# A one-core decoder layer: activation blocks stored 288 columns apart instead of 264, in 21 shared buffers instead of 23

## The chip, the cores and the metric

The kernel runs on one core of a Trainium2 chip. The metric is the device time of one execution in microseconds (us). Three runs of the kernel before took 2701.3, 2703.62 and 2700.91 us, so the median is 2701.3 us.

## What is computed

One layer of a hybrid decoder on 264 tokens: 256 of a prompt and 8 single tokens of running requests, all with 2,048 features and in float32. The reference, cut to what matters:

```python
def layer_forward(x, pos, ret_state0, ret_chunk, sparse_attn, p):
    x = x + 0.5 * swiglu(rms_norm(x, ffn1_norm), ffn1_w1, ffn1_w2)
    h = rms_norm(x, mix_norm)
    rq, rk, rv, rg, aq, ak, av, iq, ik, iw, g_ret, g_att = split_cols(h @ w_in)
    ret_out, ret_state = retention(rq, rk, rv, rg, ret_state0, ...)
    att = sparse_attn(rms_norm(aq), rms_norm(ak), av, iq, iw, ik)
    merged = sigmoid(g_ret) * ret_out + sigmoid(g_att) * (att @ w_att_out)
    x = x + merged @ w_o
    x = x + 0.5 * swiglu(rms_norm(x, ffn2_norm), ffn2_w1, ffn2_w2)
    return x, ret_state, ak, av, ik
```

Every weight is read once from DRAM, and nearly all the arithmetic is the products of weights with the activations of the 264 tokens.

## The kernel before, in words

Features lie on the 128 partitions and tokens along the row, so an activation block is [128 features, 264 tokens], 1,056 bytes in each partition. Four such blocks make one **quad**, a tile [128, 4, 264] from `qpool`, a pool of `NQ` = 23 buffers that nearly every larger tile shares (`quad`, L146; `Blocks`, L166, hands out block `i` as `[:, i % 4, :]` of quad `i // 4`). The residual X (4 quads), the two halves of the normalized input of a stage (`hi` and `lo`, 4 quads each), the two halves of the hidden features of an FFN chunk (`hh`, `hl`), the quads of retention and attention (`rk`, `rq`, `vr`, `ro`, `kn`, `qn`) and, with other shapes of at most 4,100 bytes, the tiles of the decode tokens' side work (`sb`, `kq`, `kv`, `kb`, `qb`, `pr`) all come from it. A tile that wants a buffer waits until the last reader of the buffer's previous tile is done.

`mblock` (L236) multiplies 128 columns of a weight matrix with up to 16 activation blocks. For each 8 rows of blocks it loads 512 KB of weights (`wr`, SyncE's queue), rounds them on ScalarE to float32r (`wh`, L247), takes the rest on VectorE, or in some stages on GpSimd (`wl`, L248), and then issues per block k three TensorE matmuls of 264 columns: L251 with moving block `hi[k]` and weights `wh`, L252 with `lo[k]` and `wh`, L253 with `hi[k]` and `wl`. `wr`, `wh` and `wl` have four buffers each. There are 20,400 such matmuls in the program.

The stages in order: FFN 1 (`ffn`, L305: three chunks of hidden features, each all of its `w1` blocks, then all of its `w2` blocks), the combined projection (`mixblock`, in the order iq, rk, rq, rv, ak, av, aq, gr, ga, rg), the three products with `wro`, `wao` and `wo`, and FFN 2. Between the blocks of the combined projection Python generators are stepped (`step`, L411) that hold the side work: the index search, prompt attention, retention, and for the 8 decode tokens `retention_decode` (L889) and `decode_attention` (L788). `retention_decode` has 16 steps: load a state `sb` and two broadcasts `kq` on ScalarE's queue, `kv` and the update of `sb` on VectorE, a product on GpSimd (L905), a sum on VectorE (L906), and the store of `sb`. `decode_attention` has 16 half steps: a broadcast `qb` on ScalarE's queue, two products `pr` on GpSimd (L802) and their sums on VectorE (L804), with `kb` gathered once per two.

The framework's scheduler orders each engine's instructions by priority and its own estimate of time, and it decides which of the free buffers a tile gets.

In each partition's memory the pools lie one behind the other in the order in which they are made, and tiles are rounded up to 32 bytes. In the built program of before the first quad lies at byte 26,688, which is 64 past a multiple of 128. A quad takes 4,224 bytes, 33 times 128, so every quad begins 64 past a multiple of 128, and the four blocks of a quad begin 64, 96, 0 and 32 bytes past one. All `wh` and `wl` blocks (512 bytes each) begin 64 past one.

Of the kernel before, what the change touches and what calls it, by code (L numbers as in the profile page):

```python
# [9 lines left out]
F32 = mybir.dt.float32  # L10
# [6 lines left out]
PSUM = bass.MemoryType.PSUM  # L17
DRAM = bass.MemoryType.DRAM

P = 128  # L20
# [2 lines left out]
TP = 256  # L23
NB = 8
T = TP + NB
FF = 5632
FB = FF // P
CHUNKS = ((0, 16), (16, 32), (32, 44))
EPS = 1e-6
# [13 lines left out]
SW = 136  # L43
# [5 lines left out]
ORDER = (("iq", 8), ("rk", 8), ("rq", 8), ("rv", 16), ("ak", 4), ("av", 4), ("aq", 16), ("gr", 16), ("ga", 16),  # L49
         ("rg", 16))  # L50

NQ = 23
AHEAD = 1500

CC = {}
_c = 0
for _n, _w in (("ident", 128), ("cos", T), ("sin", T), ("causal", 384), ("kdec", 16), ("bm8", 8), ("rep", 128),
               ("pages", 16), ("same", 128), ("before", 128), ("eighths", 7), ("slot", 2), ("segkey", 1),
# [63 lines left out]
def layer(ctx: ExitStack, tc: tile.TileContext, xT, gains, consts, dmat, didx, pt, state, cidx, ck, cv,  # L122
# [6 lines left out]
    cpool = ctx.enter_context(tc.tile_pool(name="cpool", bufs=1))  # L129
    qpool = ctx.enter_context(tc.tile_pool(name="qpool", bufs=NQ))  # L130
    rawp = ctx.enter_context(tc.tile_pool(name="rawp", bufs=4))
    hip = ctx.enter_context(tc.tile_pool(name="hip", bufs=4))
    lop = ctx.enter_context(tc.tile_pool(name="lop", bufs=4))
    work = ctx.enter_context(tc.tile_pool(name="work", bufs=2))
# [7 lines left out]
    def nm(s):  # L142
        cnt[0] += 1
        return f"{s}_{cnt[0]}"

    def quad(dt=F32, shape=(P, 4, T), s="q"):  # L146
        return qpool.tile(list(shape), dt, tag="q", name=nm(s))

    def quads(n, dt=F32, s="q"):
        return [quad(dt, s=s) for _ in range(n)]  # L150

    def wt(s="w", shape=(P, T), dt=F32, tag="w", bufs=8):
        return work.tile(list(shape), dt, tag=tag, name=nm(s), bufs=bufs)

    def mt(s, shape=(P, 384), dt=F32):
        return work.tile(list(shape), dt, tag="m", name=nm(s), bufs=8)
# [4 lines left out]
    def aux():  # L161
        return psa.tile([P, 512], F32, tag="aux", name=nm("aux"))

    def auxm():
        return psa.tile([P, 512], F32, tag="auxm", name=nm("auxm"), bufs=1)

    class Blocks:
# [3 lines left out]
        def __getitem__(self, i):  # L171
            q = i // 4
            if q not in self.t:
                self.t[q] = quad(self.dt, s=self.s)
            return self.t[q][:, i % 4, :]
# [27 lines left out]
    nc.vector.memset(ones256, 1.0 / 256)  # L203
    ones1 = cpool.tile([P, P], F32, name="ones1")
    nc.vector.memset(ones1, 1.0)
    onesw = cpool.tile([P, SW], F32, name="onesw")
    nc.vector.memset(onesw, 1.0)
    epst = cpool.tile([P, 1], F32, name="epst")
    nc.vector.memset(epst, EPS)

    ptb = cpool.tile([P, NB, NPG], I32, name="ptb")
# [9 lines left out]

    xs = dpool.tile([P, KB, T], F32, name="xs")
    gs = dpool.tile([2, KB, P, T], F32, name="gs")
    ats = dpool.tile([P, AH, TP], F32, name="atsd")
# [3 lines left out]
    rows = dpool.tile([3, P, P], F32, name="rows")  # L228
# [7 lines left out]
    def mblock(src, nk, hi, lo, m=P):  # L236
        ps = psm.tile([P, 512], F32, tag="ps", name=nm("ps"))
        for c0 in range(0, nk, 8):
# [10 lines left out]
            for k in range(n):  # L249
                g = c0 + k  # L250
                nc.tensor.matmul(ps[:m, :T], wh[:, k, :m], hi[g], start=g == 0, stop=False)  # L251
                nc.tensor.matmul(ps[:m, :T], wh[:, k, :m], lo[g], start=False, stop=False)  # L252
# [3 lines left out]
    def root(ms, y, t):  # L256
        nc.scalar.activation(t, ms, AF.Ln)
        nc.scalar.activation(y, t, AF.Exp, scale=-0.5)

    def newton(y, ms, t):  # L260
        nc.vector.tensor_tensor(t, y, y, op=ALU.mult)
        nc.vector.scalar_tensor_tensor(t, t, -0.5, ms, op0=ALU.mult, op1=ALU.mult)
        nc.vector.scalar_tensor_tensor(y, t, 1.5, y, op0=ALU.add, op1=ALU.mult)

    def rsqrt(src, y, ms, t):
        """y = (src + EPS) ** -0.5"""
        nc.vector.tensor_scalar(ms, src, EPS, None, op0=ALU.add)
        root(ms, y, t)
        newton(y, ms, t)

    class Norm:
        """Gains and sums of squares of the blocks of x as they come; the mean's root follows at the evacuations."""

        def __init__(self, gain):
            self.gain = cc(gain)
# [17 lines left out]
        def done(self):  # L293
            ps = auxm()
            nc.tensor.matmul(ps[:, :T], onesD, self.acc, start=True, stop=True)
            ms, t = wt("ms"), wt("t")
            self.rstd = wt("rstd", tag="rstd", bufs=2)
            rsqrt(ps[:, :T], self.rstd, ms, t)
            return self.rstd
# [53 lines left out]
    ffn(norm, w1a, w2a, out1, early=1)  # L353

    KT = [[quad(shape=(P, 1024 + h), s="kt") for h in range(2)] for _ in range(4)]
    kt_order = [(p, 8 * h + i) for h in range(2) for p in range(4) for i in range(8)]

# [11 lines left out]
    blocks = {}  # L369
# [281 lines left out]
    VSELF = st([P, KVH, NB], tag="vself", bufs=1)  # L651

    def rms_roots(sums):
        """Steps from functions that give PSUM sums to the tiles of two roots each."""
        ss, y, t = (mt(n, (P, 2, T)) for n in ("ss", "y", "t"))
        for j, f in enumerate(sums):
            pq = aux()
            f(pq[:, :T])
            nc.scalar.activation(ss[:, j, :], pq[:, :T], AF.Identity, bias=epst)
        yield  # L660
        root(ss, y, t)
        yield
        newton(y, ss, t)
        yield y

    def norm_heads(raw, gain, i):
        """Normalizes two of the four heads of a quad in place."""
        sq = []
        for j in range(2):
            q = wt("sq")  # L670
            nc.scalar.activation(q, raw[:, i + j, :], AF.Square)
            sq.append(q)
        yield

        def total(j):
            return lambda pq: nc.tensor.matmul(pq, ones128, sq[j], start=True, stop=True)

        for y in rms_roots([total(0), total(1)]):
            yield
        r = raw[:, i:i + 2, :]  # L680
        nc.vector.scalar_tensor_tensor(r, r, gain, y, op0=ALU.mult, op1=ALU.mult)
        yield

    def k_task():
        for i in (0, 2):
            yield from norm_heads(KN.t[0], cc("gk"), i)
        nc.scalar.dma_start(o_k, KN.t[0])
        nc.vector.tensor_copy(KS, KN.t[0][:, :, TP:])
        yield
        KG = quad(s="kg")  # L690
        nc.scalar.activation(KG, KN.t[0], AF.Copy, scale=gqs)
        KN.t[0] = KG
        yield
# [12 lines left out]
    QR = st([P, AH, 2], tag="qr", bufs=1)  # L706

    def q_task(g):
        """Means of squares of four heads, with the tokens on the partitions."""
        pq = aux()  # L710
        for i in range(4):
            q = wt("sq")
            nc.scalar.activation(q[:, :TP], QN[4 * g + i][:, :TP], AF.Square)
            for tt in range(2):
                c = 2 * i + tt
                nc.tensor.matmul(pq[:, c:c + 1], q[:, P * tt:P * tt + P], ones128[:, :1], start=True, stop=True)
            if i % 2:
                yield
        nc.vector.tensor_copy(QSS[:, 4 * g:4 * g + 4, :].rearrange("p h t -> p (h t)"), pq[:, :8])
        nc.vector.tensor_copy(QS[:, 4 * g:4 * g + 4, :], QN.t[g][:, :, TP:])  # L720
        yield
# [151 lines left out]
        nc.gpsimd.tensor_add(out, a, b)  # L873

    def bcast_rows(src, which, scale=1.0):
        """src [128 d, (b, h)] as rows of d in DRAM, to be read onto all partitions."""
        n = src.shape[1]
        pr = auxm()
        nc.tensor.transpose(pr[:n, :P], src, ident)
        rt = mt("rt", (P, P))  # L880
        nc.scalar.activation(rt[:n], pr[:n, :P], AF.Copy, scale=scale)
        nc.scalar.dma_start(rows[which, :n], rt[:n])
# [73 lines left out]
    def group_norm():  # L956
        for hq in range(4):
            sq = {}
            for i in range(2):
                for e in range(2):  # L960
                    q = wt("sq")
                    nc.scalar.activation(q, RO[2 * (2 * hq + i) + e], AF.Square)
                    sq[i, e] = q
            yield

            def total(i):
                def f(pq):
                    for e in range(2):
                        nc.tensor.matmul(pq, ones256, sq[i, e], start=e == 0, stop=e == 1)
                return f  # L970

            for y in rms_roots([total(0), total(1)]):
                yield
            for i in range(2):
                h = 2 * hq + i
                for e in range(2):
                    nc.vector.scalar_tensor_tensor(RO[2 * h + e], RO[2 * h + e], cc("grn")[:, e:e + 1], y[:, i, :],
                                                   op0=ALU.mult, op1=ALU.mult)
            yield
# [98 lines left out]
    for i in range(16):  # L1078
# [3 lines left out]
        s = wt("s")  # L1082
# [56 lines left out]


def _blocks(w):
    """[K, M] as [M / 128, 128, K / 128, 128]: the columns' blocks, each with its rows on the partitions."""
    k, m = w.shape
    return np.ascontiguousarray(w.reshape(k // P, P, m // P, P).transpose(2, 1, 0, 3))

# [58 lines left out]
```

## Time and profile before, and how to read it

| what | value |
|---|---|
| median of three runs | 2701.3 us |
| profiled execution, its span | 2703.1 us |
| TensorE matmul busy | 2621.5 us, 97% of the span, 21,205 instructions |
| VectorE busy | 1596.6 us, 59% |
| ScalarE busy | 1163.4 us, 43% |
| GpSimd busy | 647.2 us, 24% |
| mean granted TensorE clock | 0.987 |

For the profiled execution no time of its own is given beside its span of 2703.1 us; the three runs lie within 2.8 us of one another, and the span lies 1.8 us above their median. Engines in the rows: PE is TensorE's matmuls, PEld its weight loads, DVE is VectorE, ACT ScalarE, POOL GpSimd, SP SyncE; a letter q behind a name is that engine's queue of transfers. L251 is line 251 of the kernel. The records of one matmul overlap the next ones, because matmuls are pipelined: the time that a matmul takes from the engine is read from one start to the next and not from its own duration. [...]

### The profile page before, as it was taken

How to read it: one execution, taken by the hardware profiler on the slowest of the kernel's cores; microseconds unless marked ns; L12 is line 12 of the kernel's file. 1: busy time of each engine (PE TensorE's matmuls, PEld its weight loads, DVE VectorE, ACT ScalarE, POOL GpSimd, SP SyncE). 2: the span in 40 equal slices, each digit the busy share in tenths (PEclk: the TensorE clock that was granted, in tenths of full speed). 3: DMA queues.
4: the chain of work that ended last, by engine and by line, in shares of the span. 5: the costliest groups of instructions: out<-in, count | busy, mean ns of one | idle time of the engine just before them, and what ended most of it. 6: DMA issues, size and time to landing. Idle time of an engine off the chain costs nothing.

```text
span 2703.1 us, 51188 instructions
## 1 busy us (share of the span) xinstructions
PE 2621.5 (97%) x21205; PEld 2588.8 (96%) x21205; DVE 1596.6 (59%) x2301; ACT 1163.4 (43%) x1551; POOL 647.2 (24%) x427
## 2 busy tenths in 40 slices
PE   7999999999999899999988899999999999999999
PEld 7999999999999699899988899999999999999999
DVE  6555555555566578568798845566655555554554
ACT  5443344334453333443545654444544334433443
POOL 3110011001127443445455543231111001100110
PEclk9999999999999899998998999999999999999999
DMA  6556555655566354468886666666555655566555
GB/s 216 180 181 184 181 180 181 184 182 180 173 218 214 108 170 157 141 213 282 266 291 228 203 195 223 206 208 210 180 181 182 181 183 180 180 181 183 181 166 173
DMA packets 164745, 520.67 MB, mean 193 GB/s; under 512 B 21680, under 2 KB 38640, under 8 KB 164512
## 3 DMA queue, kind: packets, MB, share of 16 engines
q1 hardware_dynamic: 126496, 445.31, 52.4%
q10 hardware_dynamic: 32112, 56.51, 6.4%
q0 software_dynamic: 5904, 15.59, 1.8%
q8 instruction: 166, 2.72, 0.4%
q14 instruction: 67, 0.55, 0.1%
HBM read 495.73 MB, written 21.60 MB: 191 GB/s over the span
## 4 chain that ended last, share of the span: by engine, by line
PE 82%; DVE 7%; issue 3%; DMA 3%; POOL 2%; ACT 2%; ACTq 0%; DVEq 0%; POOLq 0%
PE ps L252 27%; PE ps L251 26%; PE ps L253 26%; DVE wl L248 2%; DMA wr<-win 1%; POOL wl L248 1%; POOL pr L802 1%; DVE junk L534 1%; ACT wh L247 1%; DMA qb<-rows 0%; DMA kq<-rows 0%; DMA vb<-cv,rowi 0%; DVE sTs L804 0%; PE aux L443 0%; DVE sb L903 0%
## 5 line engine op out<-in xcount | busy, mean ns | idle before, releaser
L247 ACT ACTIVATE wh<-wr 128x1024 fp32r<-128x1024 f32 x866 | 902.0, 1043 | 1294.1 <-PE ps L252 838.5
L248 DVE TENSOR_TENSOR wl<-wr,wh 128x1024 fp32r<-128x1024 f32 (+2 forms) x798 | 990.3, 1241 | 740.2 <-ACT wh L247 739.1
L251 PE MATMUL ps<-hi,wh 128*128 128x264 f32 x4624 | 1326.4, 287 | 19.3 <-ACT hi L282 10.1
L253 PE MATMUL ps<-hi,wl 128*128 128x264 f32 x4624 | 1326.7, 287 | 16.2 <-DVE wl L248 13.3
L252 PE MATMUL ps<-lo,wh 128*128 128x264 f32 x4624 | 1329.2, 287 | 1.6 <-DVE lo L283 1.5
L251 PEld LDWEIGHTS ps<-hi,wh 128*128 128x128 f32 x4624 | 878.0, 190 | 23.0 <-ACT hi L282 10.1
L253 PEld LDWEIGHTS ps<-hi,wl 128*128 128x128 f32 x4624 | 876.1, 189 | 24.6 <-DVE wl L248 16.1
L252 PEld LDWEIGHTS ps<-lo,wh 128*128 128x128 f32 x4624 | 877.0, 190 | 8.7 <-issue 5.3
L322 POOL TENSOR_TENSOR s<-s,rstd 128x264 f32<-128x264 f32 x88 | 127.5, 1449 | 1252.6 <-ACT s L320 1252.6
L253 PE MATMUL ps<-hh,wl 128*128 128x264 f32 x1408 | 399.0, 283 | 0.0
L252 PE MATMUL ps<-hl,wh 128*128 128x264 f32 x1408 | 398.7, 283 | 0.0
L251 PE MATMUL ps<-hh,wh 128*128 128x264 f32 x1408 | 398.5, 283 | 0.0
L252 PEld LDWEIGHTS ps<-hl,wh 128*128 128x128 f32 x1408 | 264.7, 188 | 0.0
L251 PEld LDWEIGHTS ps<-hh,wh 128*128 128x128 f32 x1408 | 264.6, 188 | 0.0
L253 PEld LDWEIGHTS ps<-hh,wl 128*128 128x128 f32 x1408 | 264.4, 188 | 0.0
L248 POOL TENSOR_TENSOR wl<-wr,wh 128x1024 fp32r<-128x1024 f32 x68 | 170.2, 2508 | 289.9 <-ACT wh L247 250.4
L802 POOL TENSOR_TENSOR pr<-qb,kb 128x1024 f32<-128x1024 f32 x32 | 93.4, 2937 | 57.9 <-DMA qb<-rows 23.5
L291 POOL TENSOR_TENSOR acc<-acc,sq 128x264 f32<-128x264 f32 x45 | 40.5, 900 | 153.7 <-ACT sq L290 152.7
L329 DVE TENSOR_TENSOR h<-ps,s 128x264 f32<-128x264 f32 x88 | 38.0, 432 | 66.0 <-PE ps L253 62.7
L362 POOL DMA_INDIRECT kt<-cidx,kix x64 | 71.9, 1123 | 19.1 <-issue 18.5
L252 PE MATMUL ps<-mlo,wh 128*128 128x264 f32 x256 | 72.9, 285 | 0.0
L252 PE MATMUL ps<-alo,wh 128*128 128x264 f32 x256 | 72.7, 284 | 0.0
(311 smaller groups left out, 2270.0 us busy)
## 6 DMA issues: line engine op xcount, KB each, us to landing
wr<-win SPq DMA_DIRECT2D x224, 512.0 KB, 4.4
wr<-w1a SPq DMA_DIRECT2D x176, 512.0 KB, 3.8
wr<-w1b SPq DMA_DIRECT2D x176, 512.0 KB, 3.7
wr<-w2a SPq DMA_DIRECT2D x80, 512.0 KB, 3.7
wr<-w2b SPq DMA_DIRECT2D x80, 512.0 KB, 3.6
wr<-wro SPq DMA_DIRECT2D x32, 512.0 KB, 4.8
wr<-wao SPq DMA_DIRECT2D x32, 512.0 KB, 4.9
wr<-wo SPq DMA_DIRECT2D x32, 512.0 KB, 3.9
```

Source lines behind the costliest of these rows:

```text
L247: nc.scalar.activation(wh[:, :n, :m], wr[:, :n, :m], AF.Copy)
L248: eng.tensor_sub(wl[:, :n, :m], wr[:, :n, :m], wh[:, :n, :m])
L251: nc.tensor.matmul(ps[:m, :T], wh[:, k, :m], hi[g], start=g == 0, stop=False)
L252: nc.tensor.matmul(ps[:m, :T], wh[:, k, :m], lo[g], start=False, stop=False)
L253: nc.tensor.matmul(ps[:m, :T], wl[:, k, :m], hi[g], start=False, stop=g == nk - 1)
L291: nc.gpsimd.tensor_add(self.acc, self.acc, sq)
L322: nc.gpsimd.tensor_mul(s2, s, rstd)
L329: nc.vector.tensor_mul(h, pu, s2)
L362: nc.gpsimd.indirect_dma_start(out=KT[p][pg // 8][:, o:o + PG], out_offset=None, in_=cidx, in_offset=bass.IndirectOffsetOnAxis(ap=kix[:, p ...
L534: nc.vector.scalar_tensor_tensor(junk, VS, thr, onesw, op0=ALU.is_ge, op1=ALU.mult, accum_out=out)
L802: nc.gpsimd.tensor_mul(pr, qb, k.to_broadcast([P, 2, 4, P]))
```

## The change

`quad` without a shape now takes a tile [128, 4, 288] and hands out its first 264 columns; the pool has 21 buffers. `onesw` takes 24 columns more, and `epst` goes from `cpool` into a new pool of 64 bytes between `wr` and `wh`, which shifts the addresses of what follows. Comments between triple quotes go, without effect.

```diff
 T = TP + NB
+TS = 288
...
-NQ = 23
+NQ = 21
...
     rawp = ctx.enter_context(tc.tile_pool(name="rawp", bufs=4))
+    offp = ctx.enter_context(tc.tile_pool(name="offp", bufs=1))
     hip = ctx.enter_context(tc.tile_pool(name="hip", bufs=4))
...
-    def quad(dt=F32, shape=(P, 4, T), s="q"):
+    def quad(dt=F32, shape=None, s="q"):
+
+        if shape is None:
+            return qpool.tile([P, 4, TS], dt, tag="q", name=nm(s))[:, :, :T]
         return qpool.tile(list(shape), dt, tag="q", name=nm(s))
...
-    onesw = cpool.tile([P, SW], F32, name="onesw")
+    onesw = cpool.tile([P, SW + 24], F32, name="onesw")[:, :SW]
     nc.vector.memset(onesw, 1.0)
-    epst = cpool.tile([P, 1], F32, name="epst")
+    epst = offp.tile([P, 16], F32, name="epst")[:, :1]
```

In the built program the first quad now lies at byte 26,752, a multiple of 128, a quad takes 4,608 bytes, 36 times 128, and a block 1,152, 9 times 128. So all 20,400 moving blocks begin on a multiple of 128. The `wh` and `wl` blocks begin 64 past one, as before. Matmuls still read 264 columns.

The scheduler's order moves where quads are scarce. First ScalarE's queue in the aq stage, at the seventh and eighth of the 16 steps of `retention_decode` (sb is the state's tile, o_sts the output that it is stored to, sq belongs to attention). Before:

```order
L894 DMA sb_14360<-state 128x1024
L898 DMA kq_14362<-rows 128x512 x2
L713 ACTIVATE sq_14513<-qn_14277 128x256
L247 ACTIVATE wh_14438<-wr_14437 128x1024
L247 ACTIVATE wh_14468<-wr_14467 128x1024
L713 ACTIVATE sq_14517<-qn_14277 128x256
L894 DMA sb_14498<-state 128x1024
L898 DMA kq_14500<-rows 128x512 x2
L908 DMA o_sts<-sb_14360 128x1024
```

The same place with the change (line numbers are 5 higher):

```order
L899 DMA sb_14363<-state 128x1024
L903 DMA kq_14365<-rows 128x512 x2
L718 ACTIVATE sq_14516<-qn_14280 128x256
L252 ACTIVATE wh_14441<-wr_14440 128x1024
L252 ACTIVATE wh_14471<-wr_14470 128x1024
L718 ACTIVATE sq_14520<-qn_14280 128x256
L913 DMA o_sts<-sb_14363 128x1024
L252 ACTIVATE wh_14561<-wr_14560 128x1024
L899 DMA sb_14501<-state 128x1024
L252 ACTIVATE wh_14591<-wr_14590 128x1024
L903 DMA kq_14503<-rows 128x512 x2
```

The load of the next state moved from ahead of the store of the last one to behind it, and `kq` with it. Second, GpSimd at the eighth to eleventh step and the first products of `decode_attention` (kv and pr are the products, kb a gathered page). Before:

```order
L905 TENSOR_TENSOR kv_14503<-sb_14498,kq_14500 128x1024
L782 DMA kb_14875<-ck,rowi_12896 128x512 x2
L905 TENSOR_TENSOR kv_14716<-sb_14711,kq_14713 128x1024
L802 TENSOR_TENSOR pr_14880<-qb_14878,kb_14875 128x1024
L802 TENSOR_TENSOR pr_14883<-qb_14878,kb_14875 128x1024
L802 TENSOR_TENSOR pr_15049<-qb_15047,kb_14875 128x1024
L905 TENSOR_TENSOR kv_14891<-sb_14886,kq_14888 128x1024
L802 TENSOR_TENSOR pr_15052<-qb_15047,kb_14875 128x1024
```

With the change:

```order
L910 TENSOR_TENSOR kv_14506<-sb_14501,kq_14503 128x1024
L910 TENSOR_TENSOR kv_14719<-sb_14714,kq_14716 128x1024
L787 DMA kb_14878<-ck,rowi_12899 128x512 x2
L807 TENSOR_TENSOR pr_14883<-qb_14881,kb_14878 128x1024
L807 TENSOR_TENSOR pr_14886<-qb_14881,kb_14878 128x1024
L910 TENSOR_TENSOR kv_14894<-sb_14889,kq_14891 128x1024
L807 TENSOR_TENSOR pr_15052<-qb_15050,kb_14878 128x1024
L807 TENSOR_TENSOR pr_15055<-qb_15050,kb_14878 128x1024
```

The two kinds of products, which were interleaved one by one, now follow each other in whole pairs. SyncE's order, the weight loads, is the same in both, and so is nearly all of TensorE's.

## Rows read from the trace of the kernel before

**Rows 1.** The page: the span, and each engine's busy time, share and instructions.

```profile
span 2703.1 us, 51188 instructions
PE 2621.5 (97%) x21205; PEld 2588.8 (96%) x21205; DVE 1596.6 (59%) x2301; ACT 1163.4 (43%) x1551; POOL 647.2 (24%) x427
```

**Rows 2.** Busy time by stretch: stretch, length, engines' busy us (instructions), clock, DMA share, GB/s.

```profile
60.00:790.00 730.00, 730.00 (x6031) 730.00 (x6030) 383.13 (x446) 305.82 (x373) 70.94 (x55) 1.00 0.60 183
790.00:1530.00 740.00, 679.54 (x5180) 653.03 (x5179) 553.59 (x1050) 317.45 (x484) 377.64 (x213) 0.95 0.64 208
1530.00:2690.00 1160.00, 1157.45 (x9599) 1153.04 (x9599) 617.18 (x745) 501.69 (x632) 176.99 (x129) 1.00 0.60 189
```

**Rows 3.** TensorE in order of time, FFN 1, from a quad's first block: start, duration, what.

```profile
300.20 0.28 PE L251 MATMUL ps<-hi,wh 128*128 128x264 f32 x1
...
300.56 0.29 PE L251 MATMUL ps<-hi,wh 128*128 128x264 f32 x1
...
300.93 0.28 PE L251 MATMUL ps<-hi,wh 128*128 128x264 f32 x1
301.05 0.28 PE L252 MATMUL ps<-lo,wh 128*128 128x264 f32 x1
301.16 0.28 PE L253 MATMUL ps<-hi,wl 128*128 128x264 f32 x1
301.28 0.28 PE L251 MATMUL ps<-hi,wh 128*128 128x264 f32 x1
...
301.65 0.28 PE L251 MATMUL ps<-hi,wh 128*128 128x264 f32 x1
```

**Rows 4.** The same view, the first quad of the product with wro.

```profile
1650.42 0.28 PE L251 MATMUL ps<-rhi,wh 128*128 128x264 f32 x1
...
1650.78 0.28 PE L251 MATMUL ps<-rhi,wh 128*128 128x264 f32 x1
...
1651.14 0.29 PE L251 MATMUL ps<-rhi,wh 128*128 128x264 f32 x1
...
1651.51 0.28 PE L251 MATMUL ps<-rhi,wh 128*128 128x264 f32 x1
...
1651.86 0.28 PE L251 MATMUL ps<-rhi,wh 128*128 128x264 f32 x1
```

**Rows 5.** The same view, the first quad of the product with wo.

```profile
1836.46 0.28 PE L251 MATMUL ps<-mhi,wh 128*128 128x264 f32 x1
...
1836.83 0.29 PE L251 MATMUL ps<-mhi,wh 128*128 128x264 f32 x1
...
1837.19 0.28 PE L251 MATMUL ps<-mhi,wh 128*128 128x264 f32 x1
...
1837.54 0.28 PE L251 MATMUL ps<-mhi,wh 128*128 128x264 f32 x1
...
1837.91 0.28 PE L251 MATMUL ps<-mhi,wh 128*128 128x264 f32 x1
```

**Rows 6.** Waits from 1180 to 1530 us: who for whom, us in total, times, longest.

```profile
ACT wh L247 <- DMA wr<-win: 32.1, 10, 6.9
...
POOL pr L802 <- DMA qb<-rows: 23.5, 6, 6.8
```

**Rows 7.** The chain that ended last: start, us, what; the first load, one of qb.

```profile
1.29 8.22 DMA x<-xT
...
1333.45 8.10 DMA qb<-rows
```

**Rows 8.** ScalarE's table loads by line: busy, mean ns.

```profile
L257 ACT ACT_TABLE_LOAD x10 | 12.8, 1283 | 2.6 <-DVE qm L1056 2.5
```

## The prediction

> **What bounds the kernel now.** I read the page first: TensorE's matmuls are busy for 97% of the span, no other engine for more than 59% [rows 1]. A busy TensorE can still be a slow one, so the second view is the busy time by stretch [rows 2]. From 60 to 790 us and from 1530 to 2690 us TensorE has next to no idle time, and the clock is granted in full: 6,031 matmuls in 730.00 us are 121.0 ns each, 9,599 in 1160.00 us are 120.8 ns. Almost all of them are the 264-column kind. [...] From 790 to 1530 us it is different: 5,180 matmuls take 740 us, and TensorE is idle for 60 us of them, while VectorE is at 75%. There the side work of the decode tokens sets the pace in places.
>
> [...] By the addresses given ahead, the four blocks of a quad begin 64, 96, 0 and 32 bytes past a multiple of 128, and each block is the moving operand of three matmuls in a row. From the first matmul of one block to that of the next, a quad in FFN 1 takes 0.36, 0.37, 0.35 and 0.37 us [rows 3]: the third block, the only one on a multiple of 128, is the quickest. In the product with wo it is 0.37, 0.36, 0.35, 0.37 [rows 5]. In the product with wro it is 0.36, 0.36, 0.37, 0.35 [rows 4]: there the aligned block is the slowest. Starts are given to 0.01 us, so the error of one such difference is as large as the differences; what speaks is that two of three places agree.
>
> **The change, part by part.** *All moving blocks on a multiple of 128.* The three aligned blocks took 0.35, 0.37 and 0.35 us, a mean of 0.357 us or 118.9 ns a matmul. Against the 121.0 ns of the stretches that is 2.1 ns. The bounds: if the FFN 1 block is what every block becomes, 0.35 / 3 = 116.7 ns, a gain of 4.3 ns; if the wro block is, 0.37 / 3 = 123.3 ns, a loss of 2.3 ns. I take the mean, since nothing in the rows says which of the three a program of aligned blocks alone is like. In the two stretches with a busy TensorE there are 15,630 matmuls: 15,630 x 2.1 ns = 32.8 us. Of the 5,180 between, I count half as on the path, since TensorE is near 92% busy there but waits for the side work at its ends: 2,590 x 2.1 = 5.4 us. Together 38 us less. Loading and splitting weights must keep up: VectorE is at 52% and 53%, ScalarE at 42% and 43%, DMA at 60% in those stretches [rows 2], so a TensorE that is 2% faster meets no other engine.
>
> *23 buffers become 21.* In an FFN the residual, the two halves of the input and the two halves of a chunk hold 4 + 8 + 8 = 20 quads. The first two quads of the next chunk then find one free buffer instead of three, but the last readers of the old ones are matmuls that stand ahead on TensorE anyway, so I cost this at nothing; what hides it is TensorE's own order. It differs around 1180 to 1530 us. With the normalized input (8), RO (4), QN (up to 4), the scaled keys and the values (2) held, 5 of 23 buffers are left for `sb`, `kq`, `kv`, `kb`, `qb`, `pr`; of 21 only 3. The order shows it: the load of a state moves behind the store of the last one, and GpSimd's products no longer alternate. What waits is ScalarE's queue, and behind the waiting transfer stand the roundings `wh`, and behind those `wl` and the matmuls. The price of one exposed load is that of qb, 8.1 us [rows 7]. Seven steps of `retention_decode` lie in the stretch where `decode_attention` wants buffers too, so the cost lies between nothing (the four `wh` buffers cover 11.6 us of TensorE, four times 24 matmuls of 121 ns) and 7 x 8.1 = 57 us. That side work already waits here for loads, 23.5 us at `pr` alone, and the roundings wait 32.1 us for weights [rows 6]. I take one exposed load, 8 us: nearer to nothing, because the order moves each load by a few roundings and not by a step.
>
> *The loads of x and the spills.* A quad's rows are no longer contiguous, so a transfer of 4,224 bytes in a partition becomes four of 1,056. The first load of x is on the path at the start with 8.22 us [rows 7]. Bounds: nothing, if the bytes set its time, and another 8.2 us if it doubles. I take 1 us, since the bytes are the same. The later spills and reloads run beside TensorE.
>
> *The rest.* ScalarE's order holds five more table loads, 1.28 us each [rows 8], 6.4 us on an engine that is idle for 422 of the 740 us in that stretch; nothing. The padding of `onesw` and the move of `epst` issue nothing. If that cover is gone, it is 6.4 us.
>
> **The sum.** 2703.1 - 38 + 8 + 1 = 2674 us for the profiled execution, which lies 1.8 us above the median of the runs: **2672 us**.
>
> **The rivals.** *R1, every block as quick as the aligned one in FFN 1.* For it: two of three places [rows 3, 5], and no block then follows a misaligned one. Against it: [rows 4]. 15,630 x 4.3 ns = 67 us and half of 5,180, 11 us: 2703.1 - 78 + 9 - 1.8 = 2632 us. Chance 0.22.
>
> *R2, the change of place does not change the rate.* Quads in the rows take 1.45 us however the four blocks share it: 1.45 in [rows 3], 1.44 in [rows 4], 1.45 in [rows 5], and the stretches agree to 0.2 ns a matmul. A quick block may only get back what its neighbours lost. The wro quad is also the one whose two halves lie a multiple of 256 bytes apart, as all do after the change (a quad is then 18 times 256). Then nothing is won, and the two costs remain, from 0 to 9 us and a little more: 2701 to 2712 us. [...] Chance 0.23.
>
> *R3, the buffers decide.* The mechanism is ScalarE's queue: a load of `sb` that waits for the store of the last state holds up `wh`, and with it TensorE. From more than about five exposed loads on (38 / 8.1 = 4.7) it eats the gain. With all seven: 2701.3 - 38 + 57 + 1 = 2721 us, slower. Chance 0.08.
>
> *R4, aligned blocks are slow when they are alone.* As in [rows 4] every block takes 0.37 us: 15,630 x 2.3 + 2,590 x 2.3 = 42 us more, and 9 us: 2752 us. Chance 0.07.
>
> [...]
>
> **How the numbers follow.** The forecast has 0.37, R1 0.22, R2 0.23, R3 0.08, R4 0.07, R5 0.03. The forecast's own range, with the buffers costing 0 to 25 us, is 2660 to 2690 us. The range that holds 8 in 10 takes in R1 with a little below and the lower part of R2's costs and above: 2620 to 2714 us; R5, R4 and most of R3 stay out. A measurement of this kernel tells about 0.2%, 5.4 us. Faster by more: the forecast, R1 and R5, and a little of R2: 0.64. Within: half of R2, 0.12. Slower: the rest of R2, R3 and R4, with a part of the forecast whose buffers cost more: 0.24.
>
> **What would show it.** In the stretches of FFN 1 and 2 the matmuls per us: 8.26 before, 8.41 in the forecast, 8.57 with R1, the same with R2, fewer with R4. TensorE in order of time: four equal blocks of a quad, 0.357 us each, and no block at 0.37. From 1180 to 1530 us: waits of ScalarE's `wh` for stores of `sb` (o_sts) in the forecast about 8 us, with R3 over 40. At the start, the load of x at 8 to 10 us. The forecast is wrong if the blocks of a quad still differ, if the matmuls per us do not move, or if the stretch from 790 to 1530 us gets longer by more than 15 us.

## The result, and the profile after

Four runs of the changed kernel took 2722.05 to 2728.57 us, median 2726.58 us; the kernel before took 2702.46 us (median of four) beside it. The ratio is 1.0081, its 95% interval 1.0067 to 1.0095: **24 us slower**, where 29 us faster was forecast (2672 us against 2701.3). That is above the range's upper end of 2714 us. The page of the changed kernel, to be held against [rows 1]:

```profile
span 2723.8 us, 51226 instructions
PE 2619.0 (96%) x21205; PEld 2585.5 (95%) x21205; DVE 1605.2 (59%) x2301; ACT 1169.0 (43%) x1556; POOL 640.9 (24%) x427
```

Engines are as busy as before, and the span is 20.7 us longer: the time went into waiting. Where it went is read from the matmuls that fit into the same stretches. Busy time by stretch, first of the changed kernel, then of the kernel before (stretch, length, TensorE's busy us and matmuls, weight loads, VectorE, ScalarE, GpSimd, granted TensorE clock with 1.00 for the full one, DMA share, GB/s):

```profile
60.00:790.00 730.00, 730.00 (x6030) 730.00 (x6029) 382.26 (x444) 305.62 (x372) 70.95 (x55) 1.00 0.61 183
790.00:1290.00 500.00, 465.37 (x3622) 445.34 (x3621) 339.68 (x776) 197.43 (x286) 236.59 (x151) 0.97 0.57 185
1290.00:1530.00 240.00, 197.89 (x1455) 191.62 (x1454) 204.24 (x251) 116.99 (x193) 118.68 (x54) 0.91 0.72 238
1530.00:1680.00 150.00, 140.68 (x1201) 135.09 (x1200) 82.20 (x149) 79.41 (x127) 65.93 (x47) 0.99 0.62 204
1700.00:2690.00 990.00, 990.00 (x8175) 989.93 (x8175) 533.24 (x596) 415.53 (x499) 122.20 (x88) 1.00 0.60 187
```

```profile
790.00:1290.00 500.00, 469.06 (x3612) 448.85 (x3611) 343.02 (x780) 197.75 (x285) 242.78 (x154) 0.97 0.58 186
1290.00:1530.00 240.00, 210.48 (x1571) 204.18 (x1570) 210.57 (x271) 119.70 (x200) 134.86 (x59) 0.93 0.77 254
1530.00:1680.00 150.00, 147.45 (x1282) 143.10 (x1282) 75.12 (x137) 79.60 (x126) 55.07 (x41) 1.00 0.63 203
1700.00:2690.00 990.00, 990.00 (x8154) 989.93 (x8153) 531.34 (x596) 413.69 (x496) 117.12 (x86) 1.00 0.60 187
```

In FFN 1 nothing moved: 6,030 matmuls against 6,031 in [rows 2], 121.1 ns each against 121.0. From 1290 to 1530 us there are 116 matmuls fewer, from 1530 to 1680 us 81 fewer; at 121 ns these are 14.0 and 9.8 us lost. From 790 to 1290 us ten more fit in, and in FFN 2 twenty-one more: 1.2 and 2.5 us won. The sum, 20.1 us, is the growth of the span to within 0.6 us. So the whole loss lies in the stretch where the decode tokens' side work runs, and where buffers are scarce.

The four blocks of a quad in FFN 1, TensorE in order of time, as in [rows 3]:

```profile
300.79 0.28 PE L256 MATMUL ps<-hi,wh 128*128 128x264 f32 x1
...
301.15 0.28 PE L256 MATMUL ps<-hi,wh 128*128 128x264 f32 x1
...
301.51 0.28 PE L256 MATMUL ps<-hi,wh 128*128 128x264 f32 x1
...
301.88 0.28 PE L256 MATMUL ps<-hi,wh 128*128 128x264 f32 x1
...
302.24 0.28 PE L256 MATMUL ps<-hi,wh 128*128 128x264 f32 x1
```

0.36, 0.36, 0.37 and 0.36 us: the blocks are equal now, to the 0.01 us of the starts, as the alignment lets one expect, but equal at the old mean. 1.45 us for the quad, as before. Over 82 quads in a row from there the four blocks take 120.6 to 121.7 ns a matmul in the changed kernel; over 82 quads from the first of [rows 3] they take 121.7, 121.7, 117.2 and 123.9 ns in the kernel before. The mean is 121.1 ns in both. (The rounding of the starts leaves an error of about 1 ns in such a mean by place.) So the third block of [rows 3] was quick indeed, and the others paid for it.

Waits from 1290 to 1530 us (who for whom: us in total, times, longest), changed kernel, then the kernel before:

```profile
POOL kv L910 <- DVE sb L908: 48.8, 7, 12.4
...
POOL pr L807 <- DMA qb<-rows: 41.3, 10, 9.9
...
PE ps L258 <- DVE wl L253: 16.7, 12, 4.1
...
DVE kv L906 <- DMA kq<-rows: 13.9, 7, 3.8
...
PE aux L974 <- ACT sq L967: 12.9, 1, 12.9
ACT sq L967 <- DVE ro L916: 10.3, 1, 10.3
...
PE ps L256 <- ACT wh L252: 8.6, 2, 6.2
```

```profile
POOL kv L905 <- DVE sb L903: 18.5, 3, 8.3
...
PE ps L253 <- DVE wl L248: 10.0, 7, 3.7
...
PE aux L969 <- ACT sq L962: 2.1, 1, 2.1
...
DVE kv L901 <- DMA kq<-rows: 0.8, 1, 0.8
```

GpSimd waits for the updated state (`sb`) 48.8 us instead of 18.5, for `qb` 41.3 instead of 23.5 [rows 6], VectorE for `kq` 13.9 instead of 0.8: the steps of the side work overlap less. (In all GpSimd is idle for 121 us of these 240 instead of 105; part of its longer waits were waits for something else before.) TensorE has no part in these steps until it needs a result. The largest single wait is there: the matmuls of the group norm (L974) need `ro`, which the fifteenth of the sixteen steps completes for half of the heads, and TensorE stands still for 12.9 us before them. The last sums of the two generators (`rd` of `retention_decode`, `sTs` of `decode_attention`; first and last start), before and after:

```profile
L906 DVE TENSOR_REDUCE rd<-kv x16: 1204/1207/1223, 1199.0 to 1449.1; 128x8 f32<-128x1024 f32 x16
...
L804 DVE TENSOR_REDUCE sTs<-pr x32: 1201/1206/1220, 1317.1 to 1523.5; 128x8 f32<-128x1024 f32 x32
```

```profile
L911 DVE TENSOR_REDUCE rd<-kv x16: 1204/1207/1223, 1200.3 to 1463.2; 128x8 f32<-128x1024 f32 x16
...
L809 DVE TENSOR_REDUCE sTs<-pr x32: 1197/1204/1221, 1317.7 to 1545.2; 128x8 f32<-128x1024 f32 x32
```

Both begin when they did and end 14 and 22 us later. The product with wro begins 23.0 us later (1673.4 us against 1650.4), and from there on nothing more is lost.

### The profile page after: what moved, and what is told of

Same layout as the page of the kernel before. It is cut to its first block, busy times and chain, and to the rows that moved or that the text cites. A ratio compares the mean times of both kernels' runs of the same rounds, so it can differ in the third digit from the quotient of the medians.

```text
span 2723.8 us, 51226 instructions
## 1 busy us (share of the span) xinstructions
PE 2619.0 (96%) x21205; PEld 2585.5 (95%) x21205; DVE 1605.2 (59%) x2301; ACT 1169.0 (43%) x1556; POOL 640.9 (24%) x427
## 3 DMA queue, kind: packets, MB, share of 16 engines
q10 hardware_dynamic: 35952, 56.51, 6.5%
q0 software_dynamic: 5904, 15.59, 1.7%
## 5 line engine op out<-in xcount | busy, mean ns | idle before, releaser
L807 POOL TENSOR_TENSOR pr<-qb,kb 128x1024 f32<-128x1024 f32 x32 | 86.9, 2734 | 56.0 <-DMA qb<-rows 48.4
```

Source lines behind the costliest of these rows:

```text
L807: nc.gpsimd.tensor_mul(pr, qb, k.to_broadcast([P, 2, 4, P]))
```

## The experiments

Times of the runs e1 to e11 stand beside 2703 to 2705 us of the kernel before on the same chip. From e12 on the chips were others, on which the kernel before itself took 2749 us (e12 to e15) and 2737 us (e16 to e18). In e13 much of the difference lies between 790 and 1280 us, where it does 3,244 matmuls at a mean granted clock of 0.93 and e1 does 3,557 at 0.97. There only ratios are read, and between runs on different chips of the others too.

### Buffers or layout: e1 to e4

e1, e2 and e3 change one number in the kernel before:

```diff
-NQ = 23
+NQ = 21      (e1; 22 in e2, 24 in e3)
```

e4 changes it in the changed kernel:

```diff
-NQ = 21
+NQ = 22
```

> The kernel before with 21 buffers of 4,224 bytes instead of 23, nothing else; blocks stay 264 columns apart. Theory A (the buffers cost the time, the layout changes nothing or wins a few us): the stretch from 1290 to 1510 us grows by about 22 us as in the changed kernel, 2722 to 2730 us in all, and GpSimd's waits at pr and kv double. Theory B (the padded layout itself costs the time, by its transfers or by the matmuls): near 2702 us.

> The kernel before with 22 buffers. Theory A with a cost by the buffer: half way, 2708 to 2718 us. Theory A with a threshold (the fourth free buffer is the one that is missed): 2701 to 2705 us, or as with 21. Theory C (not the number but the accident of the schedule's order decides): no order among 21, 22, 23 and 24 buffers.

> The kernel before with 24 buffers, one more than before; it fits in the 264-column layout. Theory A: faster than 2702 us by up to the step from 22 to 23, 2690 to 2700 us. Theory B: the same, 2702 us. Theory C: anything from 2690 to 2725 us.

> The changed kernel with 22 buffers of 4,608 bytes instead of 21; the order of instructions is all but the same as in the run with 22 buffers of 4,224 bytes, so the difference of those two is the layout alone. Theory A: within 6 us of that run, below it rather (the matmuls of FFN 2 ran at 120.8 ns before, and at about 0.2 ns less in the changed kernel, 2 to 4 us). Theory B: some 20 us above it. A gain as I forecast from alignment, 38 us, would be seen here without the cost of the buffers: it is not expected any more.

| kernel | us | ratio, 95% interval | last `sTs` | wro begins |
|---|---|---|---|---|
| 264 columns, 23 buffers (before) | 2703.8 | 1 | 1523.5 | 1650.4 |
| 288 columns, 21 (the change) | 2726.6 | 1.0081 [1.0067, 1.0095] | 1545.2 | 1673.4 |
| e1: 264 columns, 21 | 2726.7 | 1.0079 [1.0066, 1.0093] | 1543.4 | 1669.5 |
| e2: 264 columns, 22 | 2716.0 | 1.0037 [1.0024, 1.0051] | 1538.3 | 1670.6 |
| e4: 288 columns, 22 | 2721.6 | 1.0064 [1.0051, 1.0078] | 1529.1 | 1659.4 |
| e3: 264 columns, 24 | 2704.8 | 1.0007 [0.9998, 1.0016] | 1509.7 | 1649.0 |

(The change was measured beside 2702.5 us. The last two columns are us in the one profiled execution, which for e2 lies above and for e4 below the median of its runs.) e1 settles it: without padding or alignment, the two missing buffers alone give the changed kernel's time, 1.0079 against 1.0081. Theory B falls, and that the times follow the number of buffers speaks against the accident of theory C. One buffer fewer costs about half. A 24th wins nothing, where theory A had 2690 to 2700 us: the side work then ends 14 us sooner, and TensorE does not gain by it. What TensorE needed of the side work it has in time with 23. With 22 buffers the padded layout (e4) is 6 us slower than e2 by the medians, where theory A had it rather below; the two intervals just touch, and where the 6 us come from stays open.

### Does the place of a block matter at all: e8, e11, e12

e8 puts 32 bytes more in front of the quads of the changed kernel:

```diff
-    onesw = cpool.tile([P, SW + 24], F32, name="onesw")[:, :SW]
+    onesw = cpool.tile([P, SW + 32], F32, name="onesw")[:, :SW]
```

> The changed kernel (288 columns, 21 buffers) with 32 bytes more in front of the quads, so that all 20,400 moving blocks begin 32 bytes past a multiple of 128 and none on one. Theory neutral (the place of a block does not set the rate; quick blocks gave back what slow neighbours took): 6,030 matmuls in the stretch from 60 to 790 us again, 121.0 ns each, and 2722 to 2731 us in all. Theory place (a block on a multiple of 128 is quicker than one at 32, as 119.4 to 122.2 ns by place in the kernel before would have it): 5,975 matmuls or fewer, and 2740 us or more.

2728.1 us, ratio 1.0086 [1.0069, 1.0102]. (The blocks of `wh` and `wl` lie behind the quads and move by 32 bytes too, from 64 to 96 past a multiple of 128.) FFN 1 in e8 (all moving blocks at 32), and below it in e1 (264 columns, blocks at 0, 32, 64 and 96), the same view:

```profile
60.00:790.00 730.00, 730.00 (x6030) 730.00 (x6029) 382.31 (x444) 305.63 (x372) 70.98 (x55) 1.00 0.60 183
```

```profile
60.00:790.00 730.00, 730.00 (x6030) 730.00 (x6029) 382.99 (x446) 305.70 (x373) 70.92 (x55) 1.00 0.61 183
```

All at 0, all at 32, and mixed: 6,030, 6,030 and 6,030 matmuls. From 1700 to 2690 us the two equal layouts have 8,175 each and e1 has 8,167, but that is no effect of the layout: other kernels with mixed blocks have 8,154 (the one before) to 8,187 (e2). Nor does the rest of the program tell the layouts apart. From the first matmul of the product with wro to the end it takes 1048.9 to 1052.9 us in the nine kernels with 264 columns up to e10, and 1050.3 or 1050.4 us in the three with 288. The quick block of [rows 3] was quick at its neighbours' cost.

e11 and e12 shorten two of the three matmuls of each block in the changed kernel, and so leave the corrections out for a part of the tokens:

```diff
-                nc.tensor.matmul(ps[:m, :T], wh[:, k, :m], lo[g], start=False, stop=False)
-                nc.tensor.matmul(ps[:m, :T], wl[:, k, :m], hi[g], start=False, stop=g == nk - 1)
+                nc.tensor.matmul(ps[:m, :TP], wh[:, k, :m], lo[g][:, :TP], start=False, stop=False)
+                nc.tensor.matmul(ps[:m, :TP], wl[:, k, :m], hi[g][:, :TP], start=False, stop=g == nk - 1)
```

(TP is 256; e12 has P, 128, in its place.)

> The changed kernel with two of the three matmuls of each block (the corrections, lo with wh and hi with wl) reading 256 columns instead of 264: the corrections of the eight decode tokens are left out. [...] If the array takes a fixed time by the column (121.1 / 264): 118.65 ns, 6,152 matmuls. If whole lines of 128 bytes count (nine for 264 columns, eight for 256): (121.1 + 2 x 107.6) / 3 = 112.1 ns, 6,510 matmuls, and this would be the one way in which the place of a block could matter. If a matmul's issue sets the rate: 121.1 ns, 6,030 matmuls.

> As the run with 256 columns, but the two corrections read 128 columns: they are left out for the second half of the prompt and the decode tokens. [...] If a pair of weight load and matmul has a floor near 119 ns whatever its columns, 119 to 121 ns, and 6,030 to 6,130 matmuls from 60 to 790 us. If the second, narrower moving operand is read at a slower rate, 200 ns and more.

e11 took 2706.2 us. FFN 1 in e11, then in e12, busy time by stretch:

```profile
60.00:790.00 730.00, 730.00 (x6085) 729.93 (x6084) 387.20 (x450) 309.74 (x377) 71.64 (x56) 1.00 0.61 185
```

```profile
60.00:790.00 730.00, 721.99 (x6292) 721.05 (x6291) 400.28 (x467) 320.04 (x388) 92.55 (x77) 0.99 0.64 194
```

e11: 730.00 / 6,085 = 120.0 ns. If the long matmul still takes 121.1, the short ones take 119.4 ns: eight columns saved 1.6 ns, less than half of the 3.7 ns that are eight 264ths of 121.1. None of the three expectations holds. e12: 721.99 / 6,292 = 114.7 ns for a mean of 173 columns: a third of the columns gone, 5% of the time saved, at a mean granted clock of 0.99. Of its two expectations the floor near 119 ns comes nearer, and neither holds. (From 790 to 1530 us the mean granted clock in e12 is 0.63, against 0.95 in [rows 2], and its whole, 2852 us and more, tells nothing of a matmul.) But 115 ns is no floor under every pair of a weight load and its matmul. The 48 matmuls of the narrow product with `wik` have weights of 80 columns instead of 128. The first of them in e12, and the first of the sixteenth group of three, TensorE in order of time:

```profile
750.54 0.30 PE L256 MATMUL ps<-hi,wh 128*80 128x264 f32 x1
...
754.51 0.30 PE L256 MATMUL ps<-hi,wh 128*80 128x264 f32 x1
```

45 starts in 3.97 us, 88 ns a matmul, with the same moving columns as the 114.7 ns: in e12 the matmuls with 80 weight columns are 27 ns quicker than those with 128. With 264 moving columns in all three of a group they are not. The same 48 matmuls in the changed kernel (first and last):

```profile
789.11 0.28 PE L256 MATMUL ps<-hi,wh 128*80 128x264 f32 x1
...
794.80 0.28 PE L258 MATMUL ps<-hi,wl 128*80 128x264 f32 x1
```

5.69 us for 47 starts, 121.1 ns, as with 128 weight columns. And a place in the changed kernel where the granted clock is 0.50, after 2.4 us in which TensorE stood waiting for gathered pages:

```profile
1604.90:1606.90 2.00, 2.00 (x11) 2.00 (x10) 0.58 (x8) 0.22 (x1) 2.00 (x1) 0.50 0.07 29
```

```profile
1605.00 0.42 PE L258 MATMUL ps<-hi,wl 128*128 128x264 f32 x1
1605.22 0.42 PE L256 MATMUL ps<-hi,wh 128*128 128x264 f32 x1
1605.44 0.42 PE L257 MATMUL ps<-lo,wh 128*128 128x264 f32 x1
1605.66 0.42 PE L258 MATMUL ps<-hi,wl 128*128 128x264 f32 x1
```

The first row is busy time by stretch, the four below it are TensorE in order of time. Nine starts from 1604.78 to 1606.76 us give 220.0 ns from start to start, with all blocks on a multiple of 128; in the kernel before, with blocks at all four places, the starts at this clock are 0.22 us apart too (from 983.30 us on). So at the half clock the place of a block does not show either. At the full clock the matmul takes 121.1 ns, 11.1 ns more than half of 220.0. If all of the 121.1 ns went with the clock, it would be 242.2 ns at the half clock; so a part of it does not. How large that part is, and what it is, is not shown. The weights' columns show where the moving blocks are short (88 against 114.7 ns in e12) and not at 264 (121.1 ns with 80 as with 128). What sets 121.1 ns there stays open.

### What the missing buffers do: e5, e6, e7, e9, e10

All but e10 have 21 shared buffers and 264 columns, that is e1 with one more edit. e5 gives the states two buffers of their own, e6 the broadcasts `qb`, from a pool beside `qpool`:

```diff
+    ownp = ctx.enter_context(tc.tile_pool(name="ownp", bufs=2))
...
-                sb = quad(shape=(P, 4, 2, P), s="sb")
+                sb = ownp.tile([P, 4, 2, P], F32, tag="sb", name=nm("sb"))
```

> 21 shared buffers (264 columns), and besides them two buffers of 4,096 bytes in a pool of their own for the states sb of retention_decode. Theory S (the steps of retention_decode are the chain that is late; each state holds its buffer from its load to the end of its store): back to 2700 to 2709 us, and TensorE's wait for the group norm's squares falls from 13 to about 2 us. Theory Q (the products of decode_attention are what lacks buffers): stays at 2720 to 2728 us. Theory N (only the number of buffers counts): 2700 to 2709 us here and in the next run.

> The same with the two extra buffers for the broadcasts qb of decode_attention. Theory S: little gained, 2715 to 2728 us. Theory Q: 2700 to 2709 us. Theory N: 2700 to 2709 us in both.

e5: 2716.6 us, 1.0035 [1.0024, 1.0046]. e6: 2718.7 us, 1.0051 [1.0036, 1.0066]. Each gives back 8 to 12 of the 22 us, and no theory had said so: neither kind of tile alone is the late one, and the number of buffers is not all that counts, since 21 + 2 is not as good as 23 shared.

What a load waits for can be read from the trace: it goes out right behind the last reader of the buffer's previous tile. The changed kernel at the eleventh and twelfth step, VectorE, GpSimd and ScalarE's queue in order of time:

```profile
1341.65 1.22 DVE L809 TENSOR_REDUCE sTs<-pr 128x8 f32<-128x1024 f32 x1 [3.48 <-POOL pr L807]
1342.91 0.34 ACTq L899 DMA_DIRECT2D sb<-state  x1
...
1354.07 3.26 POOL L910 TENSOR_TENSOR kv<-sb,kq 128x1024 f32<-128x1024 f32 x1 [4.66 <-DVE sb L908]
1357.36 0.33 ACTq L803 DMA_DIRECT2D qb<-rows  x1
...
1365.71 1.22 DVE L809 TENSOR_REDUCE sTs<-pr 128x8 f32<-128x1024 f32 x1 [2.65 <-POOL pr L807]
1366.96 0.34 ACTq L899 DMA_DIRECT2D sb<-state  x1
```

The state is loaded 0.04 us after a sum of `decode_attention` has read its product `pr` (1341.65 + 1.22), and the next `qb` of `decode_attention` 0.03 us after GpSimd's product of that state. At these steps the two generators wait for each other in turn. The loads of five states in a row, the tenth to the fourteenth, begin 0.03 to 0.04 us after such a sum, in the changed kernel and in e1. In the built program of the changed kernel these five states lie in buffers that a `pr` had before. In the kernel before no state's load does so; those of the eleventh to the thirteenth step follow their own generator:

```profile
1327.31 2.40 POOL L905 TENSOR_TENSOR kv<-sb,kq 128x1024 f32<-128x1024 f32 x1
1329.74 0.34 ACTq L894 DMA_DIRECT2D sb<-state  x1
...
1345.68 2.39 POOL L905 TENSOR_TENSOR kv<-sb,kq 128x1024 f32<-128x1024 f32 x1
1348.10 0.34 ACTq L894 DMA_DIRECT2D sb<-state  x1
```

GpSimd's product of the tenth step is on time in the changed kernel; those of the eleventh to the fourteenth are 8, 17, 22 and 26 us late. That is where the lateness arises. How much of the 22 us the turns are worth is not shown: in e2, e5 and e6 no state's load follows such a sum, and they are still 9 to 14 us slower than the kernel before by the ratios.

e7 and e9 move what waits. e7 delays the group norm, e9 the end of `decode_attention` too; e10 is e9's edit with 23 buffers.

```diff
-        step(a=1.3, b=0.8, c=1.7)
+        step(a=1.3, b=0.8, c=2.3 if i > 3 else 0)                           (e7)
+        step(a=1.3, b=0.8 if i < 10 else 0.2, c=2.2 if i > 3 else 0.5)      (e9, e10)
```

> 21 shared buffers (264 columns), and the steps of group_norm begin four blocks later in the ga stage (none in the first four, then 2.3 a block instead of 1.7 from the start). If TensorE's wait for the group norm's squares (12.9 us in the changed kernel) is lost time in itself, 2712 to 2717 us; if it only shows a lateness that TensorE would meet elsewhere (at the roundings, or where ro is needed in the rg stage), 2722 to 2730 us.

> 21 shared buffers (264 columns); in the ga stage both group_norm and the end of decode_attention come later: c is 0.5 for four blocks and then 2.2, b is 0.8 for ten blocks and then 0.2 (1 in the rg stage, as before). In the run with the norm alone TensorE stood 15.6 us before the scores of decode_attention instead of 12.9 us before the norm, and was not behind the kernel before until then. Theory T (the side work is some 20 us late with 21 buffers, and it costs TensorE only where an instruction that needs it stands too early in TensorE's order): both waits go, 2700 to 2710 us. Theory L (the side work is a chain that sets the end of this stretch wherever its results are asked for): the wait moves once more, into the rg stage or to wro, 2720 to 2732 us.

> The kernel before (23 buffers, 264 columns) with the same two rates. Theory T: nothing to win but its 2.1 us before the norm and what the rg stage no longer waits for, 2695 to 2705 us. If the later end of decode_attention crowds the rg stage: 2706 to 2720 us.

e7: 2730.9 us, 1.0103 [1.0084, 1.0123], no better than e1. TensorE's waits in e7 from 1290 to 1560 us begin with

```profile
PE aux L812 <- DVE sTs L808: 15.6, 1, 15.6
```

The wait before the norm is gone, and TensorE stands as long where it next asks for the side work, at the scores of `decode_attention`. e9 moves that place away as well. 2719.6 us, 1.0061 [1.0047, 1.0074]: by the ratios 5 us better than e1, with intervals that overlap, and both waits are gone. Where the rest went, e9 by stretch:

```profile
1290.00:1530.00 240.00, 209.75 (x1571) 204.33 (x1570) 210.28 (x261) 123.24 (x202) 119.96 (x52) 0.94 0.73 243
1530.00:1680.00 150.00, 138.96 (x1153) 131.81 (x1153) 90.15 (x145) 76.37 (x123) 71.09 (x51) 0.97 0.62 202
```

From 1290 to 1530 us e9 does 1,571 matmuls, exactly as many as the kernel before; from 1530 to 1680 us it does 129 fewer, 15.6 us. Most of the loss moved one stage further instead of going, as theory L had it; the last `sTs` is now at 1558.3 us. e10, the same rates with 23 buffers, took 2700.8 us, 0.9995 [0.9986, 1.0004]: the later steps cost nothing where the side work is in time.

### Fewer buffers wanted: e13 to e18

In e13 (21 buffers), e14 (23) and e15 (23, with e9's rates) the second product of a half step is written over `qb`, so that a half step holds one buffer less. e16 joins this with e5; e17 (264 columns) and e18 (288 columns) have it with 22 buffers.

```diff
-                    pr = quad(shape=(P, 2, 4, P), s="pr")
+                    pr = quad(shape=(P, 2, 4, P), s="pr") if tt == 0 else qb
```

> 21 shared buffers (264 columns); the second product of each half step of decode_attention is written over qb instead of into a buffer of its own, so a half step takes two buffers and not three. Theory K (side work is late because its steps wait for buffers, and what counts is buffers wanted times the time they are held): 10 to 20 us less than with 21 buffers, 2706 to 2717 us. Theory L2 (the load and product latencies of a step set it, buffers only through the schedule's order): 2718 to 2728 us.

> The kernel before (23 buffers) with the same edit. 23 and 24 buffers took the same time, so by theory K nothing is left to win: 2698 to 2706 us. In place the second product waits for the first one's reading of qb, on one engine in order, so nothing is lost either.

> The kernel before with both: the product in place, and the later steps in the ga stage (c 0.5 for four blocks and then 2.2, b 0.8 for ten blocks and then 0.2). The later steps alone gave 0.9995 of the kernel before. If the waits that are left are of the side work's buffers: 2690 to 2699 us; if not, 2697 to 2706 us.

> 21 shared buffers (264 columns) with both reliefs: two buffers of their own for the states sb, and the second product of a half step of decode_attention in place. Theory K: as many buffers for the side work as 23 give, so the ratio to the kernel before is 0.998 to 1.002. Theory accident: about half again, 1.003 to 1.005.

> 22 buffers of 4,224 bytes (264 columns), the second product in place. Theory K: one relief on top of one buffer, 0.999 to 1.002.

> The changed kernel's layout (288 columns, blocks on multiples of 128) with 22 buffers, the second product in place; the order of instructions is the last run's but for some twenty places at the start. If the layout is neutral: within 0.0015 of the last run. If it costs, as between the runs with 22 buffers: 0.002 to 0.003 above it. If it wins as its matmuls in FFN 2 let one think: up to 0.001 below it.

| run | ratio, 95% interval |
|---|---|
| e13: 21 buffers, in place | 1.0030 [1.0009, 1.0051] |
| e14: 23 buffers, in place | 1.0016 [0.9993, 1.0038] |
| e15: 23 buffers, in place, later steps | 1.0000 [0.9981, 1.0018] |
| e16: 21 buffers, own `sb`, in place | 1.0045 [1.0013, 1.0078] |
| e17: 22 buffers, in place | 1.0017 [0.9983, 1.0051] |
| e18: 288 columns, 22 buffers, in place | 1.0011 [0.9968, 1.0055] |

e13 gives back more than half of e1's 1.0079 (0.0030 is left) with no byte more of memory, as theory K said. e14 and e15 win nothing with 23 buffers, as theory K also had it. e16 speaks against K: two reliefs should have brought it to 0.998 to 1.002, and its interval, though wide, leaves out all of that but the upper end. So the number of buffers decides, and the reliefs are not shown to add; as the framework's scheduler places every instruction anew in each of these kernels, no price of a single tile follows from them. e17 and e18 are the third pair that differs by the layout: 288 columns against 264 is +0.0002 with 21 buffers, +0.0027 with 22, and -0.0006 here. With intervals of 0.003 and 0.004 to either side the last pair cannot tell 0 from 0.0027; by the medians of all its twelve runs each it is +0.0006. So no gain of the layout shows in any pair, and a small loss with 22 buffers is neither shown nor ruled out. No version beat the kernel before by more than its measurement tells.

## Why the prediction was wrong, point by point

- **Alignment, 38 us less: the step that failed.** It measured 0: 6,030 matmuls in FFN 1 whatever the place, and no difference behind it that stands out. The step took the time of the aligned block of a quad (a mean of 118.9 ns over three quads) as the pace of a program made of such blocks. The rows ahead already spoke against it: the three quads took 1.45, 1.44 and 1.45 us however their blocks shared it [rows 3 to 5]. That was rival R2, at 0.23, and it is right in its mechanism (e1, e8, and the 82 quads). The deeper error is to read the differences between the blocks of a quad as time that the place of each sets. The same matmul at the half clock, where no place is quicker, could have been looked up in the trace before: from 983.30 us on, at a granted clock of 0.50, it has thirteen starts in a row 0.22 us apart. What sets the 121.1 ns at the full clock stays open.
- **23 buffers to 21, 8 us: mis-sized, it measured 22** (e1: 0.0079 of 2703.8 us is 21.4 us; the medians differ by 22.9). The upper bound, 57 us, held it; rival R3, at 0.08, priced its own case at 2721 us. That this lies near the result is luck: it has 38 us of gain that did not come and 57 us of cost that were 22. R3's mechanism as it was put, roundings held up behind a load that waits for the last state's store, is not what the trace shows. From 1180 to 1530 us no wait of ScalarE's roundings in the changed kernel is put down to a store of `sb` (2.0 us before), and 8.3 us to the update of `sb` that such a store ahead of them waits for (7.7 us before). Its wider form is there, a transfer on ScalarE's queue that waits for a buffer. The load of the twelfth state goes out at 1366.96 us after ScalarE stood idle for 4 us, without a wait of TensorE behind it; behind that of `qb` at 1357.36 us TensorE waits 2.9 us for `pts`. But TensorE's longest wait for a rounding, 6.2 us before 1417.41 us, is for one that stands behind a sigmoid that waits for VectorE. What is late is the chain of the steps on GpSimd and VectorE, whose loads wait in turn for the other generator's tiles; TensorE pays at the first place in its order that needs the chain's end, and at `wl` and `wh`. Nor is the move of a load behind the store, which the order ahead shows for the seventh and eighth step, the place of the loss: at the eleventh to the fourteenth step the load stands behind the last state's store in both kernels, 5 to 9 us behind it before and 12 to 15 us in the changed kernel. I took one exposed load because the order moved each load by a few roundings; the order does not show what a load waits for.
- **Load of x, 1 us: right.** The first rounding of x begins at 10.3 us instead of 9.5, the last at 23.4 instead of 22.9. Four transfers for one is what ScalarE's queue shows, not the load of x: the page counts 35,952 packets there (q10) instead of 32,112 (three more for each of the 128 partitions in ten transfers of a quad), and 5,904 on GpSimd's queue (q0), which carries that load, in both kernels.
- **Table loads, 0: right** as far as the rows tell. ScalarE is busy for 314 of the 740 us from 790 on, and TensorE's waits name no table load.
- **What would show it** was well chosen. The matmuls per us of FFN 1 did not move, and the stretch from 790 to 1530 us got longer by more than 15 us (the transposes of the scores at its end come at 1548.0 us instead of 1529.4); either was to count against the forecast.

The answer is R2's rate with a price of the buffers between the forecast's 8 us and R3's 57. The prediction had given each rival a case of its own and none to the two together; with what was measured that is 2701 + 22 + 1 = 2724 us, 3 us below what came.

## What to carry to other kernels

Before a layout is changed for a faster inner instruction, find out what sets its pace: sum the starts over a whole group and not over one member of it, and look the same instruction up at another clock or with other sizes in the same trace. When a change pays with buffers, look at the most crowded stretch of the program and count how many are left there for tiles that come and go. Look which instruction a late load goes out right behind: it is the reader that the buffer was waiting for. Then ask which instruction of the bound engine needs the end of that chain. Moving that instruction alone mostly moves the loss, as e7 and e9 show.

## What was not expected of the hardware

A float32r matmul of 264 columns takes 121.1 ns from start to start at the full clock whether its block begins at 0 or at 32 past a multiple of 128 (the changed kernel and e8), and with 80 weight columns as with 128. Shortening two of three matmuls to 256 columns leaves a mean of 120.0 ns (e11), to 128 columns 114.7 ns with 128 weight columns and 88 ns with 80 (e12). At a granted clock of 0.50 the matmul of 264 columns takes 220.0 ns, and not twice 121.1.
